# Moving the residual loads, the head stacks and one norm factor within the sliding-window stage of a decoder layer

## The chip, the cores and the metric

The kernel runs on one core of one Trainium2 chip. The time is the device time of one execution in microseconds (us), and the figure that counts is the median of several executions. PE is the matmul engine, DVE the vector engine, ACT the scalar engine, POOL the fourth compute engine, and SP the engine whose queue issues nearly all DMA transfers here. Every engine takes its own instructions strictly in order and waits for others by semaphores.

## The reference

One decoder layer on 512 tokens of width 2048, all in float32:

```
h = RMSNorm(x);  [sb_q|sb_k|sb_v|sw_q|sw_k|sw_v] = h @ w_in
A: 16 heads, causal stick-breaking attention over 512 keys
B: 16 query heads on 4 key heads, window of 128 keys, ALiBi slopes, one learned sink per head
x = x + concat(RMSNorm_A(outA), RMSNorm_B(outB)) @ w_out
x = x + SwiGLU(RMSNorm(x));  out = RMSNorm(x)
```

`outA` and `outB` are 1024 wide each, so `w_out` has a first half of rows that meets `outA` and a second half that meets `outB`. The factor of `RMSNorm_A` is one number per token and can be applied after the product.

## The kernel before

**How products are made.** Float32 operands are split into a rounded high part and the rest (`hi`, `lo`), and each product is three matmuls: hi by hi, hi by lo, lo by hi. A weight tile (a *slab*, 128 x 1024 numbers) is loaded into one of three `raw` buffers by SP, copied to `whi` by ACT (line 219) and subtracted to `wlo` by DVE (line 220).

**The queue of slabs.** All dense products stand in a list `queue`; one entry is one slab with its matmul triples. `step()` emits the next triple; at the first triple of a slab it makes the slab's split and calls its `pre`, and at the third it emits the loads of the next two slabs and the split of the next. `pull(ns)` emits triples until an estimated time is used up, `drain(mark)` emits up to a mark. The attention stages call `pull` between their own steps, so that dense matmuls fill PE while the softmax runs on ACT and DVE. The order of the instructions on each engine is fixed when the program is built; DMA issues keep the order in which the code wrote them.

**The stage around the change.** After the 16 heads of A (64 jobs, lines 952 to 966) come the 16 jobs of B: four *groups* of heads g = 0 to 3, four blocks of 128 queries each. The dense work that fills them is, in the order of the list: four slabs of the value projection V (`add_swv`, on 256-wide matmuls), four slabs of queries for group 2 and four for group 3 (`add_swq`), and then the first half of the output projection in four column *parts* c = 0 to 3 (`add_outA`), four slabs each with 24 matmuls of 512 columns. A part adds its residual: a tile `x2[c]` of 128 x 2048 numbers (1 MB) is loaded from x, and line 1040 adds the part's products to it, scaled by `rstdA`, one DVE instruction for each of four token tiles. The second half (`add_outB`) follows after all jobs.

**A job** (lines 1140 to 1155) has these steps: `swa_exp` (DVE lines 1074 to 1084, ACT lines 1088 and 1089) on the scores of this job; `swa_tr` of the job before (PE transposes line 1110, ACT line 1113, DVE line 1114); `swa_av` of two jobs before (PE lines 1123 and 1124, ACT line 710, DVE line 712); `swa_norm` (DVE lines 1094 to 1102, ACT line 1100); `swa_scores` of the next job (PE lines 1059 and 1060, eight 256-wide matmuls).

**Stacks.** Before its scores a group needs its keys and queries stacked as hi and lo halves: `stack_two` is one ACT and three DVE instructions (lines 696 to 699), `stack_one` one ACT and one DVE instruction (lines 705, 706). `kst[0]` serves groups 0 and 1, `kst[1]` groups 2 and 3.

**Who frees what.** The pool `v8` has four tiles of 8 KB per partition. They hold first the values of A, then the stacks `kst` and `qst`, then the four residual tiles. A residual tile takes the place of a stack, so its load waits until the last scores that read the stack are done: `x2[0]` waits for block 3 of group 1, `x2[1]` for block 3 of group 2, `x2[2]` for block 3 of group 3, and `x2[3]` for nothing more.

**`rstdA`** is the norm factor of A (`sumsq_rstd`): eight small matmuls on the sums of squares `sqA` (line 725), and nine small instructions of DVE and ACT (lines 728 and 276 to 286). It is made between the jobs of A and those of B.

Of the kernel before, what the change touches and what calls it, by code (L numbers as in the profile page):

```python
# [8 lines left out]
F32 = mybir.dt.float32  # L9
# [7 lines left out]
P = 128  # L17
# [20 lines left out]
def tile_hymba(ctx: ExitStack, tc: tile.TileContext, x, ln_mix, w_in, sb_norm, swa_norm,  # L38
# [42 lines left out]
    def four(c):  # L81
        return [pz() for _ in range(NT)] if c % 2 == 0 else [pm(), pm(), po(), po()]
# [639 lines left out]
    def sumsq_rstd(acc, name):  # L722
        pb = po()
        for t in range(NT):
            mm(pb[:, 2 * t:2 * t + 2], lhsT=acc[:, t * P:(t + 1) * P], rhs=ones[:, 0:2],
               start=(t == 0), stop=True, skip_group_check=True)
        sst = sm.tile([P, NT], F32, tag="sst", name="sst")
        V.tensor_copy(out=sst, in_=pb[:, 0:2 * NT].rearrange("p (t two) -> p t two", two=2)[:, :, 0])
        return rstd_from(sst, NT, 1.0 / SBW, name)
# [15 lines left out]
    def sbt(dt, name, n=512, bufs=1):  # L745
        return phase[1].tile([P, n], dt, tag=name, name=name, bufs=bufs)
# [59 lines left out]
    drain_to(11, 0)  # L806
    oA = [o8.tile([P, 4, 512], F32, tag="o8", name="oA") for _ in range(2)]
    kqs = ExitStack()
    kq2 = kqs.enter_context(tc.tile_pool(name="kq2", bufs=1, side="right", reuse_waits="tile")).tile([P, 2, 512], F32, name="kq2")
    add_feat(win, [(C_SWK, 256)], two_m, lambda c, pb: k_evac(pb, kq2[:, c, :]))  # L810
    sb_mark = len(queue)
    add_swv()
# [2 lines left out]
    for name in ("sh3", "sl3", "wh3", "wl3"):  # L815
        z3[name] = sbt(F32R, name, 256)
        G.memset(f(z3[name]), 0.0)
    sqA = sbt(F32, "sqA")

    class Head:  # L820
        pass
# [122 lines left out]
    def at(fn, j):  # L944
        if 0 <= j < NJ:
            fn(*jobs[j])
# [18 lines left out]
        at(sb_lo, j)  # L965
        pull(SBFILL / 3, sb_mark)
    drain(sb_mark)
    rstdA = sumsq_rstd(sqA, "rstdA")


    swp = open_phase("swp", 15)
# [10 lines left out]
    kst = [None, None]  # L982
    qst = [None] * 4

    def stack_keys(c):
        for e in range(2):
            stack_two(kq2[:, c, :], e * HD, kst[c][:, 2 * e, :], kst[c][:, 2 * e + 1, :])

    def stack_queries(g, src):
        for c in range(2):  # L990
            for e in range(2):
                stack_one(src[:, c, :], e * HD, qst[g][:, c * 2 + e, :])

    smarks = [0] * 4

# [10 lines left out]
        smarks[g] = len(queue)  # L1006

    kst[0], qst[0], qst[1], kst[1] = (v8.tile([P, 4, 512], F32R, tag="v8", name=n) for n in ("kst", "qst", "qst", "kst"))
    stack_keys(0)
    stack_queries(0, kq[0][:, 0:2, :])  # L1010
    for g in (2, 3):
        add_swq(g)

# [16 lines left out]
    x2 = [None] * 4  # L1030

    def add_outA(c):
        def banks():
            x2[c] = v8.tile([P, NT, 512], F32, tag="v8", name="x2")
            dma(out=x2[c], in_=x2d[:, c * 512:(c + 1) * 512].rearrange("(t p) c -> p t c", p=P))
            return four(1)

        def done(t, pb):
            xc = x2[c][:, t, :]
            V.scalar_tensor_tensor(out=xc, in0=pb, scalar=rstdA[:, t:t + 1], in1=xc, op0=ALU.mult, op1=ALU.add)  # L1040
        add_tok(lambda s: wout[s * 256:(s + 1) * 256, c * 512:(c + 1) * 512], 4, 2, 512,
                lambda k: mixA[k], banks, done, mix_prep(mixA, oA, 32))

    for c in range(4):
        add_outA(c)
# [87 lines left out]
    blks = {}  # L1133
    jobs = [(g, blk) for g in range(4) for blk in range(NT)]
    NJ = len(jobs)
    SWFILL = 6900.0
    pull(8000.0)
    at(swa_scores, 0)
    stack_queries(1, kq[0][:, 2:4, :])
    for j in range(NJ + 2):  # L1140
        at(swa_exp, j)
        pull(SWFILL / 4)
        at(swa_tr, j - 1)
        pull(SWFILL / 4)
        if j == 2:
            drain(swv_end)
        if j == 3:
            stack_keys(1)
        if j + 1 < NJ and jobs[j + 1][1] == 0:
            drain(smarks[jobs[j + 1][0]])  # L1150
        at(swa_av, j - 2)
        pull(SWFILL / 4)
        at(swa_norm, j)
        at(swa_scores, j + 1)
        pull(SWFILL / 4)
    kqs.close()
    drain()
    rstdB = sumsq_rstd(sqB, "rstdB")


# [687 lines left out]
```

## Time and profile before

| | |
|---|---|
| median of 3 runs | 2029.74 us (2028.69 to 2030.48) |
| the profiled execution's own time | 2027.9 us |
| its span | 2026.2 us |
| PE busy | 1997.1 us, 99% of the span |
| DVE, ACT busy | 1499.1 and 1504.0 us, 74% each |
| last product of A's norm factor to last product of B's (line 725, twice) | 432.85 to 638.72 us |

Times in a profile are from the start of the span. A timeline row gives start, length, engine, line and operands, and in brackets how long the engine had been idle and what ended that. A matmul's length overlaps that of the next, so its cost is the distance between two starts. In a row of the windows, each engine's busy time in the stretch stands with its number of instructions, and after them the TensorE clock granted (1.00 is full speed).

### The profile page before, as it was taken

How to read it: one execution, taken by the hardware profiler on the slowest of the kernel's cores; microseconds unless marked ns; L12 is line 12 of the kernel's file. 1: busy time of each engine (PE TensorE's matmuls, PEld its weight loads, DVE VectorE, ACT ScalarE, POOL GpSimd, SP SyncE). 2: the span in 40 equal slices, each digit the busy share in tenths (PEclk: the TensorE clock that was granted, in tenths of full speed). 3: DMA queues.
4: the chain of work that ended last, by engine and by line, in shares of the span. 5: the costliest groups of instructions: out<-in, count | busy, mean ns of one | idle time of the engine just before them, and what ended most of it. 6: DMA issues, size and time to landing. Idle time of an engine off the chain costs nothing.

```text
span 2026.2 us, 29383 instructions
## 1 busy us (share of the span) xinstructions
PE 1997.1 (99%) x10364; PEld 1703.6 (84%) x10364; DVE 1499.1 (74%) x2038; ACT 1504.0 (74%) x2063; POOL 1104.2 (54%) x597
## 2 busy tenths in 40 slices
PE   9999999989989999999999999999999999999998
PEld 8888888888868888888888888888888888888886
DVE  6667888878864787777777777777777867767767
ACT  6766777766752468777777777777777788878887
POOL 2842444420000047666676666666766678878883
PEclk9999999999989999999999999999999999999999
DMA  6422222212233354544435445354453743533423
GB/s 205 139 60 77 63 67 69 63 53 63 79 118 127 115 177 110 141 107 128 130 105 141 109 126 134 101 141 112 123 137 100 268 161 104 174 138 104 171 89 115
DMA packets 284323, 240.24 MB, mean 119 GB/s; under 512 B 11024, under 2 KB 233296, under 8 KB 281744
## 3 DMA queue, kind: packets, MB, share of 16 engines
q1 hardware_dynamic: 283504, 235.71, 39.0%
q8 instruction: 82, 1.34, 0.3%
q0 software_dynamic: 288, 1.32, 0.2%
q10 hardware_dynamic: 384, 1.34, 0.2%
q14 instruction: 65, 0.53, 0.1%
HBM read 218.40 MB, written 19.92 MB: 118 GB/s over the span
## 4 chain that ended last, share of the span: by engine, by line
PE 74%; DVE 2%; ACT 1%; DMA 1%; issue 0%; POOL 0%; DVEq 0%; ACTq 0%; POOLq 0%
PE o L118 34%; PE m L118 28%; PE m L381 2%; PE m L380 2%; PE m L382 2%; PE o L380 1%; PE o L381 1%; PE o L382 1%; PE z L118 1%; DMA raw<-in_w_out_dram 1%; PE z L1110 0%; PE o L414 0%; PE o L412 0%; PE o L413 0%; PE z L1184 0%
## 5 line engine op out<-in xcount | busy, mean ns | idle before, releaser
L118 DVE TENSOR_TENSOR wlo<-t,hp 128x1024 fp32r<-128x1024 f32 x247 | 301.1, 1219 | 184.9 <-PE o L118 114.3
L118 POOL TENSOR_TENSOR t<-raw,t 128x1024 f32<-128x1024 f32 x111 | 282.5, 2545 | 281.1 <-ACT hp L118 268.9
L118 ACT ACTIVATE whi<-t 128x1024 fp32r<-128x1024 f32 x247 | 262.0, 1061 | 125.9 <-PE o L118 76.0
L118 PE MATMUL o<-hca,whi 128*128 128x512 f32 x880 | 307.6, 391 | 0.0
L118 POOL TENSOR_TENSOR t<-raw,raw 128x1024 f32<-128x1024 f32 x114 | 295.1, 2591 | 22.2 <-issue 11.2
L118 DVE TENSOR_TENSOR wlo<-raw,hp 128x1024 fp32r<-128x1024 f32 x187 | 228.3, 1221 | 91.2 <-issue 51.7
L118 ACT ACTIVATE whi<-raw 128x1024 fp32r<-128x1024 f32 (+1 forms) x189 | 199.8, 1057 | 105.5 <-PE m L118 75.2
L118 ACT ACTIVATE hp<-t 128x1024 fp32r<-128x1024 f32 x247 | 249.1, 1009 | 2.4 <-POOL t L118 2.4
L118 PE MATMUL o<-hca,wlo 128*128 128x256 f32 x880 | 244.3, 280 | 0.0
L118 ACT ACTIVATE hp<-raw 128x1024 fp32r<-128x1024 f32 x191 | 192.8, 1009 | 3.1 <-DVE wlo L118 1.3
L118 PEld LDWEIGHTS o<-hca,whi 128*128 128x128 f32 x880 | 164.3, 187 | 35.5
L118 PE MATMUL m<-hca,whi 128*128 128x512 f32 x528 | 186.4, 392 | 1.1 <-DVE hca L118 1.1
L118 PEld LDWEIGHTS o<-hca,wlo 128*128 128x128 f32 x880 | 165.9, 189 | 0.4
L220 DVE TENSOR_TENSOR wlo<-raw,whi 128x1024 fp32r<-128x1024 f32 x87 | 109.0, 1253 | 72.5 <-ACT whi L219 71.7
L219 ACT ACTIVATE whi<-raw 128x1024 fp32r<-128x1024 f32 x87 | 91.7, 1055 | 94.2 <-PE o L382 45.8
L118 PE MATMUL m<-whi,dca 128*128 128x512 f32 x592 | 146.9, 389 | 0.0
L118 PE MATMUL o<-whi,dca 128*128 128x512 f32 x592 | 146.9, 389 | 0.0
L118 PE MATMUL m<-hca,wlo 128*128 128x256 f32 x528 | 146.5, 280 | 0.0
L412 PE MATMUL m<-hhi,whi 128*128 128x512 f32 x320 | 131.3, 410 | 0.0
L118 PEld LDWEIGHTS o<-whi,dca 128*128 128x128 f32 x592 | 111.1, 188 | 23.1
L118 PEld LDWEIGHTS m<-whi,dca 128*128 128x128 f32 x592 | 111.1, 188 | 23.1
L118 PE MATMUL m<-hcs,whi 128*128 128x512 f32 x352 | 125.9, 392 | 0.0
(386 smaller groups left out, 5265.4 us busy)
## 6 DMA issues: line engine op xcount, KB each, us to landing
raw<-in_w_gate_up_dram SPq DMA_DIRECT2D x348, 256.0 KB, 5.2
raw<-in_w_down_dram SPq DMA_DIRECT2D x68, 512.0 KB, 4.9
raw<-in_w_in_dram SPq DMA_DIRECT2D x35, 512.0 KB, 3.9
raw<-in_w_in_dram SPq DMA_DIRECT2D x66, 256.0 KB, 3.3
raw<-in_w_out_dram SPq DMA_DIRECT2D x32, 512.0 KB, 6.4
aT<-w SPq DMA_DIRECT2D x44, 256.0 KB, 3.4
xd<-aT SPq DMA_DIRECT2D x10, 1024.0 KB, 7.7
rx<-in_w_down_dram SPq DMA_DIRECT2D x20, 512.0 KB, 5.4
```

The lines of the kernel that those rows point to most:

```text
L118: return lambda *a, **k: tc.keep_in_program_order(fn(*a, **k))
L219: A.activation(out=hi, in_=raw, func=AF.Copy)
L220: V.tensor_tensor(out=lo, in0=raw, in1=f(hi), op=ALU.subtract)
L380: mm(o, lhsT=lh[:, sl], rhs=hi[:, j, :], start=first, stop=False, skip_group_check=halves)
L381: mm(o, lhsT=lh[:, sl], rhs=lo[:, j, :], start=False, stop=False, skip_group_check=halves)
L382: mm(o, lhsT=ll[:, sl], rhs=hi[:, j, :], start=False, stop=(k == nslab * a - 1), skip_group_check=halves)
L412: mm(o, lhsT=wh, rhs=xh, start=(k == 0), stop=False)
```

## The change

- The load of the residual tile moves from the `pre` of a part's first slab to the `pre` of its third. The banks for the products are still taken at the first.
- `stack_keys` and `stack_queries` are cut by head and by column pair. Before the first scores, only what group 0 needs is stacked; group 1's queries follow in jobs 0 and 1, the second half of `kst[0]` in job 2, and the two halves of `kst[1]` in jobs 5 and 6 (before: all of `kst[1]` in job 3).
- `rstdA` is made in job 3 and no longer between the two attention stages. `sqA` moves to a pool that outlives the jobs.
- Before the first scores, `pull(16000, ...)` emits slabs of V; the fill per job goes from 6900 to 5800 ns by the kernel's own estimate.
- The final `drain` comes ahead of closing the pool of `kq2` and `sqA`.

```diff
@@
-    kq2 = kqs.enter_context(tc.tile_pool(name="kq2", bufs=1, side="right", reuse_waits="tile")).tile([P, 2, 512], F32, name="kq2")
+    kqp = kqs.enter_context(tc.tile_pool(name="kq2", bufs=1, side="right", reuse_waits="tile"))
+    kq2 = kqp.tile([P, 2, 512], F32, name="kq2")
@@
-    sqA = sbt(F32, "sqA")
+    sqA = kqp.tile([P, 512], F32, name="sqA")
@@
     drain(sb_mark)
-    rstdA = sumsq_rstd(sqA, "rstdA")
+    pull(16000.0, swv_end - 1)
@@
-    def stack_keys(c):
+    def stack_keys(c, e):
+        stack_two(kq2[:, c, :], e * HD, kst[c][:, 2 * e, :], kst[c][:, 2 * e + 1, :])
+
+    def stack_queries(g, c):
         for e in range(2):
-            stack_two(kq2[:, c, :], e * HD, kst[c][:, 2 * e, :], kst[c][:, 2 * e + 1, :])
-
-    def stack_queries(g, src):
-        for c in range(2):
-            for e in range(2):
-                stack_one(src[:, c, :], e * HD, qst[g][:, c * 2 + e, :])
+            stack_one(kq[0][:, 2 * g + c, :], e * HD, qst[g][:, c * 2 + e, :])
@@
-    stack_keys(0)
-    stack_queries(0, kq[0][:, 0:2, :])
+    stack_keys(0, 0)
+    stack_queries(0, 0)
+    stack_queries(0, 1)
@@
     def add_outA(c):
-        def banks():
+        def residual():
             x2[c] = v8.tile([P, NT, 512], F32, tag="v8", name="x2")
             dma(out=x2[c], in_=x2d[:, c * 512:(c + 1) * 512].rearrange("(t p) c -> p t c", p=P))
-            return four(1)
@@
-                lambda k: mixA[k], banks, done, mix_prep(mixA, oA, 32))
+                lambda k: mixA[k], lambda: four(1), done, mix_prep(mixA, oA, 32))
+        queue[-2]["pre"] = residual
@@
-    SWFILL = 6900.0
+    SWFILL = 5800.0
     pull(8000.0)
     at(swa_scores, 0)
-    stack_queries(1, kq[0][:, 2:4, :])
+    stacks = {0: lambda: stack_queries(1, 0), 1: lambda: stack_queries(1, 1), 2: lambda: stack_keys(0, 1),
+              5: lambda: stack_keys(1, 0), 6: lambda: stack_keys(1, 1)}
     for j in range(NJ + 2):
         at(swa_exp, j)
+        if j == 3:
+            rstdA = sumsq_rstd(sqA, "rstdA")
+        if j in stacks:
+            stacks[j]()
...
-        if j == 3:
-            stack_keys(1)
...
-    kqs.close()
     drain()
+    kqs.close()
```

No instruction is added or taken away on any engine; they stand in another order between about 420 and 640 us of the profile.

On SP's queue, at the loads of the output projection, the rows were these (`raw` from `in_w_out` is one weight slab, `x` a residual tile):

```order
L100 DMA raw<-in_w_in_dram 128x4x256 x16
L100 DMA raw<-in_w_out_dram 128x2x512 x2
L100 DMA x_5240<-in_x_dram 128x4x512
L100 DMA raw<-in_w_out_dram 128x2x512 x4
L100 DMA x_5571<-in_x_dram 128x4x512
```

and are now:

```order
L100 DMA raw<-in_w_in_dram 128x4x256 x16
L100 DMA raw<-in_w_out_dram 128x2x512 x4
L100 DMA x_5332<-in_x_dram 128x4x512
L100 DMA raw<-in_w_out_dram 128x2x512 x4
L100 DMA x_5675<-in_x_dram 128x4x512
```

Each residual load stood behind two slabs of its own part, with the other two behind it; now all four slabs of the part stand ahead of it, and the next part's first slab behind it.

On PE, behind the last scores of group 3 (the last row of `kst` and `qst`), which free the third residual tile, there stood transposes of one job, the value products of another, and then the third slab of part 2, whose load waits behind that residual:

```order
L1060 MATMUL z<-kst,qst 128x256
L1110 MATMUL z<-ident,s 128x128 x8
L1123 MATMUL z<-phi,swv 128x512
L1124 MATMUL z<-plo,swv 128x512
L1123 MATMUL z<-phi,swv 128x512
L1124 MATMUL z<-plo,swv 128x512
L380 MATMUL m<-whi,mhi 128x512 x2
```

Now the same scores are followed by 15 matmuls of part 2's last slab, of which the first three are shown,

```order
L1060 MATMUL z<-kst,qst 128x256
L380 MATMUL m<-whi,mhi 128x512
L381 MATMUL m<-wlo,mhi 128x512
L382 MATMUL m<-whi,mlo 128x512
L380 MATMUL o<-whi,mhi 128x512
```

and behind those 15 by the transposes, the value products and part 3's first slab:

```order
L382 MATMUL o<-whi,mlo 128x512
L1110 MATMUL z<-ident,s 128x128 x8
L1123 MATMUL z<-phi,swv 128x512
L1124 MATMUL z<-plo,swv 128x512
L1123 MATMUL z<-phi,swv 128x512
L1124 MATMUL z<-plo,swv 128x512
L380 MATMUL m<-whi,mhi 128x512 x2
```

Behind the last scores of group 2 there stood the same transposes and value products, eight scores and part 1's third slab; now 27 matmuls of part 1's own slabs, the transposes, the value products, eight scores and then part 2's first slab.

On DVE, where the jobs of B begin, the last stacks, the norm factor and the first job stood together:

```order
L706 TENSOR_TENSOR qst<-kq,qst 64x512 x3
L728 COPY sst<-o 128x4
L975 CAST dist<-disti 128x256
L276 TENSOR_SCALAR rv<-sst 128x4
L706 TENSOR_TENSOR qst<-kq,qst 64x512
L282 TENSOR_TENSOR rt<-rr 128x4
L283 TENSOR_TENSOR rt<-rt,rv 128x4
L284 TENSOR_SCALAR rt<-rt 128x4
L286 TENSOR_TENSOR rstdA<-rr,rt 128x4
L1074 SCALAR_TENSOR_TENSOR s<-dist,z 128x128 x4
```

and now the splits of five slabs stand between the last stack and the first job (`wlo`; `swv` is the value stack of V):

```order
L697 CAST kst<-kq_1425 64x512
L698 TENSOR_TENSOR kst<-kq_1425,kst 64x512
L699 CAST kst<-kst 64x512
L220 TENSOR_TENSOR wlo<-raw,whi 128x1024 x2
L272 SCALAR_TENSOR_TENSOR swv<-m,rstd_1275,swv 128x4x64 x4
L220 TENSOR_TENSOR wlo<-raw,whi 128x1024 x3
L1074 SCALAR_TENSOR_TENSOR s<-dist,z 128x128 x4
```

More of the change, by code (lines that the diff above doesn't have):

```diff
@@ L1155, in tile_hymba @@
         pull(SWFILL / 4)
+    drain()
     kqs.close()
-    drain()
     rstdB = sumsq_rstd(sqB, "rstdB")
```

## The prediction

> **What bounds the kernel now.** I read the page first, then PE's idle times in the timeline of 415 to 645 us, the stretch in which the order differs, then the chain of waits there, the windows, and DVE's groups.
>
> ```profile
> PE 1997.1 (99%) x10364; PEld 1703.6 (84%) x10364; DVE 1499.1 (74%) x2038; ACT 1504.0 (74%) x2063; POOL 1104.2 (54%) x597
> ```
>
> PE is busy for 99% of the span, and the change removes no matmul. So it can only win or lose the time in which PE waits, or works at a lower clock, inside the moved stretch. These are PE's rows there with a bracket (those behind the last jobs of A aside), and three score rows as marks:
>
> ```profile
> 432.85 1.05 PE L725 MATMUL o<-ones,sqA 128*128 128x2 f32 x8 [1.45 <-POOL sqA L720]
> 439.97 0.39 PE L381 MATMUL m<-wlo,hhi 128*128 128x256 f32 x1 [2.37 <-DVE wlo L220]
> 488.93 0.41 PE L1110 MATMUL z<-ident,s 128*128 128x128 f32 x2 [0.77 <-DVE s L1102]
> 552.23 0.28 PE L1059 MATMUL z<-kst,qst 128*128 128x256 f32 x1
> 557.01 0.39 PE L1059 MATMUL z<-kst,qst 128*128 128x256 f32 x1 [0.79 <-DVE plo L1114]
> 561.46 1.06 PE L380 MATMUL m<-whi,mhi 128*128 128x512 f32 x2 [3.71 <-ACT whi L219]
> 579.98 0.28 PE L1059 MATMUL z<-kst,qst 128*128 128x256 f32 x1
> 591.49 0.28 PE L1059 MATMUL z<-kst,qst 128*128 128x256 f32 x1
> 593.12 0.39 PE L1059 MATMUL z<-kst,qst 128*128 128x256 f32 x1 [1.00 <-DVE plo L1114]
> 598.02 1.94 PE L1110 MATMUL z<-ident,s 128*128 128x128 f32 x8 [4.16 <-DVE s L1102]
> 602.07 0.97 PE L380 MATMUL m<-whi,mhi 128*128 128x512 f32 x2 [0.40 <-ACT whi L219]
> 638.72 1.05 PE L725 MATMUL o<-ones,sqB 128*128 128x2 f32 x8 [0.39 <-POOL sqB L720]
> ```
>
> To price the losses I need what the same matmuls cost without waits. A 256-wide one costs 0.12 us and a 512-wide one 0.228 (distance of two starts), and eight transposes cost 0.87:
>
> ```profile
> 441.03 0.28 PE L381 MATMUL m<-wlo,hhi 128*128 128x256 f32 x1
> 441.15 0.28 PE L382 MATMUL m<-whi,hlo 128*128 128x256 f32 x1
> 566.59 0.39 PE L380 MATMUL m<-whi,mhi 128*128 128x512 f32 x1
> 566.82 0.39 PE L381 MATMUL m<-wlo,mhi 128*128 128x512 f32 x1
> 528.12 0.87 PE z L1110 x8
> ```
>
> Counting the matmuls between the marks in the order before gives the **loss by stretch**:
> - 432.85 to 552.23 (last scores of group 2): 366 of 512, 196 of 256 and 68 transposes make 114.4 us; the trace takes 119.4. Lost 5.0, and 1.45 in front of it.
> - 552.23 to 579.98 (scores of the second job of group 3): 74, 16 and 16 make 20.5; the trace takes 27.75. Lost 7.25.
> - 579.98 to 591.49 (last scores of group 3): 11.4 against 11.5. Lost 0.1.
> - 591.49 to 638.72: 157, 8 and 16 make 38.4; the trace takes 47.2. Lost 8.8.
>
> Together 22.6 us, of which some 1.4 is no wait: each line 725 row takes 0.9 where I counted 0.2. Most of the rest hangs on two DMA waits:
>
> ```profile
> 553.42 0.37 SPq L100 DMA_DIRECT2D x<-in_x_dram  x1
> 553.88 6.45 DMA raw<-in_w_out_dram
> 560.35 1.07 ACT whi L219
> 593.89 0.37 SPq L100 DMA_DIRECT2D x<-in_x_dram  x1
> 594.35 6.59 DMA raw<-in_w_out_dram
> 600.96 1.06 ACT whi L219
> ```
>
> SP stands at the residual until the group's last scores have freed its tile (they start at 552.23 and at 591.49 and end about 553.3 and 593.8). The weight slab queued behind it is issued only then, lands 6.5 us later, and needs 1.07 us of ACT before PE can go on. PE had 4 us of other work. Behind each wait the clock was low, too:
>
> ```profile
> core 0: us, PE busy (x) PEld busy (x) DVE busy (x) ACT busy (x) POOL busy (x), PEclk, DMA share, GB/s
> 460.00:480.00 20.00, 20.00 (x106) 16.93 (x105) 14.53 (x32) 11.88 (x25) 0.00 (x0) 1.00 0.26 80
> 480.00:500.00 20.00, 19.23 (x99) 15.97 (x98) 19.52 (x48) 16.27 (x39) 0.00 (x0) 1.00 0.18 53
> 500.00:520.00 20.00, 20.00 (x105) 16.98 (x104) 19.69 (x45) 16.20 (x39) 1.30 (x1) 1.00 0.22 72
> 553.00:565.00 12.00, 7.45 (x32) 5.52 (x32) 10.72 (x32) 8.62 (x26) 0.00 (x0) 0.86 0.71 241
> 565.00:592.00 27.00, 27.00 (x139) 22.79 (x137) 15.15 (x34) 11.76 (x27) 1.54 (x2) 1.00 0.03 11
> 592.00:606.00 14.00, 8.44 (x34) 6.42 (x33) 11.31 (x28) 10.69 (x29) 1.02 (x1) 0.76 0.64 211
> ```
>
> ```profile
> 563.60 0.63 PE L382 MATMUL m<-whi,mlo 128*128 128x512 f32 x1
> 564.03 0.63 PE L381 MATMUL m<-wlo,mhi 128*128 128x512 f32 x1
> ```
>
> The granted clock averages 0.86 and 0.76 there, and 512-wide matmuls started 0.43 us apart, half as fast as usual. That is included in the 7.25 and 8.8.
>
> **The change, part by part.**
>
> *The seam between the stages* (stacks, `rstdA`, the first `pull`). Today PE waits 1.45 us for POOL's last sum of squares, since `rstdA` stands in front of everything, and 2.37 us for a slab's `wlo`, which DVE reaches only after the stacks, the norm factor and the first job. Afterwards both are covered by V's slabs: the `wlo` tiles stand ahead of the first job on DVE, and PE reaches the first scores only after some 27 us more of dense work, by the same count. Stacks done while POOL still sums cost more than later ones:
>
> ```profile
> L706 DVE TENSOR_TENSOR qst<-kq,qst 64x512 fp32r<-64x512 f32 x4 | 3.9, 981 | 0.1
> L706 DVE TENSOR_TENSOR qst<-qf,qst 64x512 fp32r<-64x512 f32 x8 | 5.5, 685 | 0.2
> ```
>
> I take back the whole 3.8 us (at least 1.45, if DVE is late after all; POOL's sum is certainly done by job 3).
>
> *The jobs of groups 0 to 2, with less fill.* Here the change costs. From the first job's transposes to the first `wlo` of part 1 the new order has 151 DVE instructions: seven jobs' steps, eight slab splits, the moved stacks, `rstdA`, eight splits of A's output and the first residual addition. In 480 to 520 us, a like mixture, DVE was full: 93 instructions in 39.2 us, 0.42 us each. So DVE needs 63.7 us. PE has 220 matmuls of 512, 64 of 256, 48 transposes and a line 725 row: 63.9 us. Neither leads. In-order DVE then pays for every reply of ACT that comes late, and PE for DVE. Where it was as full before, 480 to 520, PE lost 0.8 us. That is the low bound. The high bound: DVE waits for ACT as it did in the first jobs (`wlo` for `whi` at line 220, and others),
>
> ```profile
> DVE wlo L220 <- ACT whi L219: 8.9, 4, 3.2
> DVE plo L1114 <- ACT phi L1113: 1.7, 1, 1.7
> ```
>
> 10.6 us in 430 to 465, less the slack that a split one slab (5.5 us) ahead gives: some 7 us with the rest. I follow the row of 480 to 520, but over 64 us at full load instead of 40 at 98%, and with stacks and the norm factor's Ln and Exp in ACT's order between the softmax steps: 3.5 us. Of the 5.0 lost before, 0.7 is the line 725 row and 2.4 the seam's, so 1.9 stood here, and 1.6 of my 3.5 is new.
>
> *The residual loads.* The wait itself stays: SP still stands at each residual until the same scores are done, and the first slab of the next part now stands behind it. New is what PE has left to do. From the end of the scores to the first matmul of that slab takes 0.1 + 0.46 (SP's issue of the residual, row to row) + 6.5 + 1.07, so 8.1 to 8.3 us.
> - Behind group 1 ten us of PE's work follow; the residual itself lands 5.3 us after issue (row below) and is needed about as late. DVE adds it in order, with softmax behind. I price this within the 3.5.
> - Behind group 2: 27 and four 512-wide matmuls, eight transposes and eight scores, 7.05 + 0.87 + 0.96 = 8.9 us. The load is covered, but ACT does the next job's four exponentials in front of `whi`, and DVE three residual additions in front of `wlo`. I take 1.3 us lost (0 to 3) in place of 7.25.
> - Behind group 3: 19 matmuls of 512 and eight transposes, 4.32 + 0.87 = 5.2 us. The slab comes 3.1 us too late. Then all four residual additions stand on DVE between the landing and the slab's `wlo`:
>
> ```profile
> DMA to landing us min/median/max: 5.1/5.3/6.7
> L1040 DVE SCALAR_TENSOR_TENSOR x<-o,rstdA,x 128x512 f32<-128x512 f32 x8 | 6.0, 747 | 2.2 <-PE o L382 2.1
> L220 DVE TENSOR_TENSOR wlo<-raw,whi 128x1024 fp32r<-128x1024 f32 x28 | 34.3, 1223 | 28.4 <-ACT whi L219 28.2
> ```
>
> 0.1 + 5.3 + 4 x 0.70 + 1.2 = 9.4 us after the scores, against 6.1 to the slab's first low-part matmul: 3.3 to 3.4 us, at most 4.7 with the 6.7 landing. After idle times of 3.71 and 4.16 us the clock was half for 3 to 5 us, at a loss of about 2; after 2.37 it was full (441.03 to 441.15 is 0.12). A wait of 3.2 lies between; I take 1.0. Together 4.4 (3.1 to 6.7) in place of 8.8 less the 1.1 that B's norm factor keeps.
>
> The Trainium skill, "TensorE: Matmul & The Clock Gate" (Part 1, the HAM clock gate), says that the clock halves after an idle window of about 3.4 us that runs freely and does not start with the wait. By that rule a wait of 3.2 us would never hold a whole window, and the 1.0 would be nothing; the times would come out 1 us lower. The 3.71, 4.16 and 2.37 above agree with it.
>
> `SWFILL` moves no work away: with less fill per job, the rest of the slabs follows behind the jobs, where PE is full anyway (565 to 592 us shows it busy throughout). The closing of the pool after `drain` issues nothing.
>
> **The sum.** Lost after: 0.7 (line 725) + 3.5 + 1.3 + 4.4 + 1.1 = 11.0 us. Before: 22.6. The gain is 11.6 us. Against the profiled execution's own 2027.9 (span 2026.2) that is 2016.3; the median of the runs lies 1.8 above that execution, so I forecast **2018 us**.
>
> **Rivals.**
> - *The seam and the jobs cost nothing* (DVE leads PE, as 14.53 of 20 us busy in 460 to 480 would allow): losses 0.7 + 0.8 + 0 + 3.1 + 1.1 = 5.7, a gain of 17, 2013 us. Against it: 151 instructions at the full rate.
> - *DVE becomes the bound*: 7 in the jobs, 3 behind group 2, 6 behind group 3: with 0.7 and 1.1, 17.8 lost, a gain of 5, 2025 us. For it: DVE's 19.5 of 20 us; against it: 0.77 us lost there.
> - *The moved wait takes the place of the old one*: the next part's slab stalls PE by 7 behind group 2 and 8 behind group 3 as today, and only the seam's 3.8 is won, less 1.6 in the jobs: 2027.5 us, no change. For it: the chain from scores to slab is unaltered. Against it: 8.9 us of work where there were 4.
> - *Slower*: DVE stands at the late residual. If the last scores of a group fall behind so that the residual lands after its part is finished, PE runs out of banks and every softmax step queues behind. From the scores 0.1 + 6.7 + 2.8 + 1.2 = 10.8 us pass, 5.6 more than the 5.2 us of cover, three times, each with 2 us of low clock: 22.8; with 7 in the jobs and 1.8 fixed it is 31.6, 9 more than today, 2039 us. It decides once DVE lies some 4 us behind PE at groups 1 and 2, where cover is 9 to 10 us. Little speaks for it.
>
> **How the numbers follow.** The forecast gets 0.54, the rivals in order 0.20, 0.13, 0.08 and 0.05. About 0.2%, 4 us, can be told from no change, so below 2025.7 counts as faster: the forecast, the first rival and most of the second, 0.86; the same 0.09; slower 0.05. The range is 2012 to 2026: the first rival's losses a little reduced, and the second rival's with 1 us more.
>
> **What would show it.** Right: no bracket over 1 us on PE between the last jobs of A and job 3; no half clock behind group 2's last scores; one wait of 3 to 4 us at part 3's first slab, ended by `whi` or by `wlo`; DVE over 95% busy from job 2 to job 9, with many PE waits under 1 us on lines 1102, 1114 and 220 that sum to 3 to 4 us. Wrong: PE waits above 2 us at parts 1 or 2 (the residual is late on DVE), or above 6 in the jobs, or none at part 3.

## The result, and the profile after

The changed kernel takes **2015.34 us** (median of 4 runs, 2014.66 to 2015.72), the kernel before 2029.59 beside it (2028.69 to 2030.48): a ratio of 0.9929, with a 95% interval of 0.9912 to 0.9947. It is 14.3 us faster; forecast were 11.6 us and 2018. Between the two profiled executions the spans differ by 12.3 us (2026.2 and 2013.9), and that is the number on which the forecast's sum can be tested, since it was made on the profiled execution.

PE's own row of the page of the changed kernel, first of all: the same instructions, 2.2 us less busy, so some 10 of the 12.3 us are waits.

```profile
PE 1994.9 (99%) x10364; PEld 1701.0 (84%) x10364; DVE 1498.8 (74%) x2038; ACT 1502.5 (75%) x2063; POOL 1101.8 (55%) x597
```

PE's timeline of the changed kernel answers to the rows that the prediction showed of before: every row with a bracket of more than 0.35 us from the last job of A on, the first row of the scores of four jobs, and the two norm factors (lines behind 809 can have a number that differs by one to three: line 1040 of the kernel before is line 1039 here).

```profile
427.57 0.50 PE L935 MATMUL o<-l,vst 128*128 128x512 f32 x1
460.07 0.28 PE L1059 MATMUL z<-kst,qst 128*128 128x256 f32 x1
483.71 0.95 PE L725 MATMUL o<-ones,sqA 128*128 128x2 f32 x8
525.24 1.10 PE L1110 MATMUL z<-ident,s 128*128 128x128 f32 x8 [0.57 <-DVE s L1102]
531.67 0.50 PE L381 MATMUL m<-wlo,mhi 128*128 128x512 f32 x1 [0.93 <-DVE wlo L220]
562.94 0.28 PE L1059 MATMUL z<-kst,qst 128*128 128x256 f32 x1
564.41 0.73 PE L380 MATMUL m<-whi,mhi 128*128 128x512 f32 x2 [0.36 <-ACT whi L219]
572.85 0.28 PE L1059 MATMUL z<-kst,qst 128*128 128x256 f32 x1
589.85 0.28 PE L1059 MATMUL z<-kst,qst 128*128 128x256 f32 x1
599.40 0.74 PE L380 MATMUL m<-whi,mhi 128*128 128x512 f32 x2 [3.20 <-ACT whi L219]
626.45 1.02 PE L725 MATMUL o<-ones,sqB 128*128 128x2 f32 x8
```

The seam has no bracket left, and neither has line 725, the norm factors. One large wait remains, 3.20 us at part 3's first slab. The loss by stretch, with the prediction's prices and the matmuls counted between the marks in each order (the marks named in the table are the changed kernel's; from 589.85 to 626.45, for example, 124 of 512, 8 of 256 and 16 transposes make 30.9 us; the trace takes 36.6):

| stretch | before, us lost | after | forecast |
|---|---|---|---|
| seam: from the last row of A's jobs; before, with the 2.37 us at V's slab | 4.1 | 0.3 | 0 |
| line 725 for A (no wait) | 0.7 | 0.7 | 0.7 |
| jobs of groups 0 to 2, with what lies behind group 1 (460.07 to 562.94) | 1.9 | 2.8 | 3.5 |
| behind group 2 (562.94 to 572.85) | 7.25 | 1.0 | 1.3 |
| 572.85 to 589.85 | 0.1 | 0.1 | 0 |
| behind group 3, to B's norm factor (589.85 to 626.45) | 8.8 | 5.7 | 4.4 + 1.1 |
| sum | 22.9 | 10.6 | 11.0 |

The difference of the sums is the 12.3 us of the spans: all of the change's effect lies in this table, none behind it.

What ends the 3.20 us wait stands in the chain of waits (start, length, what) and in SP's rows of the timeline:

```profile
591.00 0.37 SPq L100 DMA_DIRECT2D x<-in_x_dram  x1
591.46 9.54 SPq L100 DMA_DIRECT2D raw<-in_w_out_dram  x4
```

Asked of the slab issued at 591.46 alone (one of the four in that row), the trace gives:

```profile
DMA to landing us min/median/max: 6.3/6.3/6.3
```

```profile
595.75 2.08 ACT s L1088 x8
...
597.92 0.48 ACT phi L1113
598.40 0.96 ACT whi L219
```

SP issues the residual at 591.00, when group 3's last scores end, and the slab at 591.46. The slab lands 6.3 us later, at about 597.7. ACT comes to its `whi` at 598.40, directly behind the last job's exponentials and a `phi`, so ACT's order adds 0.7 us to what the load takes.

The windows show how full DVE was in the jobs,

```profile
500.00:520.00 20.00, 20.00 (x107) 17.01 (x106) 18.25 (x43) 16.09 (x42) 1.29 (x1) 1.00 0.00 1
520.00:540.00 20.00, 18.50 (x96) 15.19 (x95) 19.75 (x53) 13.86 (x35) 0.00 (x0) 1.00 0.46 158
```

(behind the window's length come PE, PEld and then DVE: 18.25 and 19.75 of 20 us), and what the clock did around the wait (PE's busy time stands behind the window's length, the granted clock behind POOL's):

```profile
597.10:600.50 3.40, 1.10 (x4) 0.67 (x4) 3.17 (x5) 3.38 (x9) 0.00 (x0) 1.00 0.80 301
600.50:603.90 3.40, 3.35 (x9) 2.57 (x9) 3.29 (x9) 0.71 (x2) 0.00 (x0) 0.50 0.58 149
603.90:607.30 3.40, 3.40 (x17) 2.80 (x16) 0.26 (x1) 0.84 (x3) 0.00 (x0) 1.00 1.02 374
```

Half clock for 3.4 us, and full again. That half-rate window alone costs 1.7 us, where 1.0 was forecast.

### The profile page after: what moved, and what is told of

Its sections match the earlier page's. It is cut to its first block, busy times and chain, and to the rows that moved or that the text cites. A ratio compares the mean times of both kernels' runs of the same rounds, so it can differ in the third digit from the quotient of the medians.

```text
span 2013.9 us, 29375 instructions
## 1 busy us (share of the span) xinstructions
PE 1994.9 (99%) x10364; PEld 1701.0 (84%) x10364; DVE 1498.8 (74%) x2038; ACT 1502.5 (75%) x2063; POOL 1101.8 (55%) x597
## 4 chain that ended last, share of the span: by engine, by line
PE 95%; DVE 2%; ACT 2%; issue 1%; DMA 0%; POOL 0%; SPq 0%; DVEq 0%; ACTq 0%; POOLq 0%
PE o L118 36%; PE m L118 30%; PE m L412 4%; PE m L413 3%; PE m L414 3%; PE m L381 2%; PE m L382 2%; PE m L380 2%; PE z L118 1%; PE o L381 1%; PE o L382 1%; PE o L380 1%; PE o L935 0%; PE o L934 0%; PE z L851 0%
```

## The experiments

Three questions were open: whether the 14 us come from the residual's place or from the seam; what exactly sets the cost of a residual load; and why the clock fell.

The experiments were run in three rounds; the kernel before, run beside them, took 2028.8, 2029.6 and 2029.6 us there, so differences of less than 1 us between kernels of different rounds mean little.

**The residual's place alone.** The kernel before with only this edit:

```diff
-        def banks():
+        def residual():
             x2[c] = v8.tile([P, NT, 512], F32, tag="v8", name="x2")
...
-            return four(1)
...
-                lambda k: mixA[k], banks, done, mix_prep(mixA, oA, 32))
+                lambda k: mixA[k], lambda: four(1), done, mix_prep(mixA, oA, 32))
+        queue[-2]["pre"] = residual
```

> The kernel before, with one part of the change alone: the residual is loaded at a part's third slab. The seam, the stacks and the fill of 6900 stay as they were. My theory (a residual load costs what the slab behind it lacks in cover): in this order the slab behind x2[1] (part 2's first) comes 12.98 us of PE work after the last scores of group 2, against 8.2 us that load and split need, so the 7.25 us lost there fall to about 0.3; the slab behind x2[2] (part 3's first) comes 4.51 us after the last scores of group 3, so a wait of about 3.8 us stays, with about 2.5 us of low clock and low-part delay, 6.4 lost in place of 8.8. The seam's 1.45 and 2.37 stay. Gain 9.4 us: 2020. Rival 1 (the seam and the spreading of the stacks bring most of the 14 us, the residual little): 2025 or more. Rival 2 (the residual brings everything): 2015.

Measured: 2019.43 us (2019.22 to 2020.9) against 2028.84, ratio 0.9956 (0.9941 to 0.9971). The gain is 9.4 us, as forecast from the covers. The seam's two waits stand as before, part 2's wait is gone, and part 3's is there with its 3.8 us:

```profile
439.86 0.51 PE L381 MATMUL m<-wlo,hhi 128*128 128x256 f32 x1 [2.38 <-DVE wlo L220]
603.41 0.91 PE L380 MATMUL m<-whi,mhi 128*128 128x512 f32 x2 [3.75 <-ACT whi L219]
```

**All the rest alone.** The changed kernel with the residual at the first slab:

```diff
-        def residual():
+        def banks():
             x2[c] = v8.tile([P, NT, 512], F32, tag="v8", name="x2")
...
+            return four(1)
...
-                lambda k: mixA[k], lambda: four(1), done, mix_prep(mixA, oA, 32))
-        queue[-2]["pre"] = residual
+                lambda k: mixA[k], banks, done, mix_prep(mixA, oA, 32))
```

> The changed kernel with the residual load put back to a part's first slab: the other parts of the change alone. My theory: the two pulls ahead of the jobs (24 us of V) bring the output projection forward, so that all three residuals come too early. The slabs behind them come 0.87, 1.90 and 1.78 us of PE work after the last scores that free the tile, against 8.2 us needed: waits of 7.3, 6.3 and 6.4 us, each with 2 us of half clock, 26 us, and some 3.5 for the rest; 29.5 lost where the kernel before loses 22.9. Slower than before by some 6 us: 2036. Rival (the parts add up: the seam is worth what the change brings beyond the residual, 4 to 5 us): 2025.

Measured: 2035.40 us (2034.21 to 2037.10), ratio 1.0034 (1.0022 to 1.0047). Slower, as the covers say. Three loads stall where two did, one per group:

```profile
524.82 0.45 PE L1110 MATMUL z<-ident,s 128*128 128x128 f32 x1 [6.33 <-DVE s L1102]
563.76 0.44 PE L1110 MATMUL z<-ident,s 128*128 128x128 f32 x1 [4.02 <-DVE s L1102]
606.05 0.45 PE L1110 MATMUL z<-ident,s 128*128 128x128 f32 x1 [4.41 <-DVE s L1102]
521.80:528.60 6.80, 3.75 (x12) 3.06 (x13) 6.70 (x17) 3.81 (x6) 0.00 (x0) 0.50 0.83 293
```

Each is followed or accompanied by 6.8 us of half clock (the last row, from the windows, is the first of the three). So the parts do not add up: the residual's place wins 9.4 alone, the rest loses 6.6 alone, and together they win 14.3. The two pulls, 24 us by the kernel's own estimate, pull the output projection forward, and the residuals with it: in the changed kernel the first scores come 32.5 us after the last row of A's jobs (427.57 to 460.07), in the kernel before 7.7 us.

**Only one pull.** The changed kernel without its second pull:

```diff
-    pull(8000.0)
     at(swa_scores, 0)
```

> The changed kernel without its second pull (8000 ns by the kernel's estimate) in front of the first scores; the 16000 stays. Everything behind the seam moves some 8 us of PE work later against the jobs. My theory: part 2's and part 3's first slabs then come some 17 and 13 us of PE work after the scores that free the tile ahead of them on SP's queue, both over 8.3, so the 5.7 us lost behind group 3 and the 1.0 behind group 2 go, and 16 us of V still cover the seam: 2015.3 - 6.4 = 2009. Rival (DVE is what holds the jobs; less fill ahead only moves the wait to another place): 2014 to 2016, with waits of PE for DVE that sum to as much. Rival 2 (the seam opens again: waits of 1 to 4 us at the first scores or at V's slabs): 2011 to 2013.

Measured: **2007.03 us** (2006.79 to 2007.83), ratio 0.9894 (0.9880 to 0.9907) to the kernel before, and 8.3 us below the changed kernel. That is 2 us more than I had forecast, and the fastest kernel of this study. Between the last job of A and B's norm factor a single wait of PE is left:

```profile
522.86 0.41 PE L1110 MATMUL z<-ident,s 128*128 128x128 f32 x2 [0.23 <-DVE s L1102]
```

The rival in which DVE holds the jobs falls with it: DVE is at 19.2, 19.7 and 19.4 of 20 us from 480 to 540 us there, against 18.3, 18.3 and 19.8 in the changed kernel, and PE loses almost nothing. In the trace the one pull puts 10.9 us ahead of the first scores (426.96 to 437.85).

**The fourth corner: one pull, and the residual at the first slab.**

```diff
-    pull(8000.0)
     at(swa_scores, 0)
...
-                lambda k: mixA[k], lambda: four(1), done, mix_prep(mixA, oA, 32))
-        queue[-2]["pre"] = residual
+                lambda k: mixA[k], banks, done, mix_prep(mixA, oA, 32))
```

> The kernel with one pull ahead of the jobs, and the residual load put back to a part's first slab: the fourth corner beside the changed kernel (2015.3), the one without the residual's move (2035.4) and the one with one pull (2007.0). My theory (loss = what the slab behind a residual lacks in cover, and the half clock behind the wait): the slabs behind the three loads come 8.88, 6.15 and 2.46 us of PE work after the scores, against 8.2 us needed: nothing, a wait of 2.1 us (perhaps with 1.7 us of half clock) and one of 5.8 us with 1.7 to 3.4 us of half clock: 11 us more than one pull, 2018 (2016 to 2020). Rival (the place of the load matters as much as it did with two pulls, 20 us): 2027. Rival 2 (with one pull the place of the load does not matter): 2007.

Measured: 2022.42 us (2021.28 to 2023.38), ratio 0.9965 (0.9951 to 0.9979). That is 4.4 us more than forecast, outside my range and about halfway to the first rival's 2027. The second and the third wait are where my theory puts them; the first was not expected:

```profile
520.64 0.73 PE L380 MATMUL m<-whi,mhi 128*128 128x512 f32 x2 [1.69 <-ACT whi L219]
556.09 0.72 PE L380 MATMUL m<-whi,mhi 128*128 128x512 f32 x2 [2.00 <-ACT whi L219]
593.20:600.10 6.90, 6.35 (x14) 4.62 (x15) 3.23 (x6) 2.90 (x7) 0.00 (x0) 0.51 0.70 232
```

The second wait is as forecast. The first, 1.69 us, was to be nothing with 8.88 us of cover; in the chain of that kernel ACT does a job's four exponentials (eight instructions with their sums) and two splits of A's output in front of the slab's `whi`:

```profile
516.36 1.22 ACT mhi L271 x2
517.58 0.79 ACT s L1088 x3
518.37 1.18 ACT s L1088 x5
519.64 0.95 ACT whi L219
```

So the 8.2 us that a slab needs behind a residual are a lower bound; ACT's order can add 2. And behind the third wait (5.01 us) the clock was half for two windows, while PE had work for 6.35 of 6.9 us.

In a table, medians in us:

| | residual at the first slab | at the third |
|---|---|---|
| before's pull (8000, behind the first scores) and fill 6900 | 2029.6 | 2019.4 |
| two pulls, fill 5800 | 2035.4 | 2015.3 (the change) |
| one pull, fill 5800 | 2022.4 | **2007.0** |

(The first row has the old seam, the others the new one.) The later load is worth about 10, 20 and 15 us.

**The fill per job.**

```diff
-    SWFILL = 5800.0
+    SWFILL = 6900.0
```

> The changed kernel with the fill per job back at 6900. My theory: the output projection runs ahead of the jobs; the slabs behind the three residuals come 2.94, 1.55 and 1.78 us of PE work after the scores, against 8.2 needed, so waits of 5.3, 6.7 and 6.4 us come back with 2 to 3 us of half clock each, although the load stands at the third slab: 2033 (2030 to 2037). Rival (the residual at the third slab is what counts, whatever the fill): 2014 to 2018, DVE having less time per job.

Measured: 2037.79 us (2036.59 to 2038.54), ratio 1.0040 (1.0025 to 1.0055). Of all edits this one moves the most: 22 us, with the residual at its new place. That is 0.8 us above the range of my theory. The waits return: 5.0 us on `whi` in three and 7.4 on line 1102 in two; two more, 2.25 us at line 1123 and 3.90 us at line 1110, are for softmax steps of DVE and ACT, and the second of them ends before the third residual is issued. The low clock after group 2 lasts 10.2 us, three times 3.4; that is where I had 2 to 3:

```profile
570.55 0.66 PE L1110 MATMUL z<-ident,s 128*128 128x128 f32 x2 [4.01 <-DVE s L1102]
569.20:579.60 10.40, 8.00 (x24) 6.42 (x25) 9.57 (x19) 6.19 (x15) 0.00 (x0) 0.51 0.75 276
```

**One slab later still.**

```diff
-        queue[-2]["pre"] = residual
+        queue[-1]["pre"] = residual
```

> The changed kernel with the residual loaded at a part's fourth slab in place of its third. The next part's first slab then stands ahead of the residual on SP's queue, its second behind. My theory (the 3.20 us wait hangs on the order of SP's queue): part 3's first slab is there in time; what PE waits for is a bank, which is free when the residual, issued at 591.0, has landed (5.1 us) and two additions are done: 597.6, a wait of about 1.6 us in place of 3.20 and no half clock; its second slab has 10.65 + 1.6 us of cover. 3.7 us won there and about 0.5 behind group 2: 2011. Rival (ACT's exponentials and DVE's additions in front of the split set the wait, not the queue): 2014 to 2015.5.

Measured: 2009.70 us (2009.59 to 2010.14), ratio 0.9902 (0.9888 to 0.9917), 5.6 us below the changed kernel. Part 3's first slab is there in time; PE now waits for a bank, which the first residual addition frees (line 1039), and the clock stays full. It waits 0.90 us where I expected 1.6, since one addition is enough:

```profile
595.45 0.50 PE L380 MATMUL m<-whi,mhi 128*128 128x512 f32 x1 [0.90 <-DVE x L1039]
```

The rival's 2014 to 2015.5 did not come. But with the slab loaded ahead of the residual its split stands ahead of the last job's exponentials, too, so this run alone does not tell SP's order from ACT's. The landing in the changed kernel does: of the 3.20 us, 0.7 are ACT's order, as shown above, and the rest is SP's queue and the load. DVE's additions add nothing there: they are done at 599.15, and the slab's `wlo` starts at 599.38, behind `whi`.

**Useless work in front of the wait.** The value products of one job, PE's last work ahead of the 3.20 us, done twice and then three times:

```diff
-        for j in range(nk):
+        for j in [j for _ in range(2 if (g, blk) == (3, 1) else 1) for j in range(nk)]:
```

> The changed kernel with useless work: the four value products of group 3's second job are computed twice (the second time starting the sum anew, so the result is the same). They are PE's last work in front of its 3.20 us wait for part 3's first slab. My theory (the 2.1 us of half clock behind that wait come of its length): 0.91 us more of work leave the end of the wait where it is, 599.40, and make the idle time 2.3 us, after which the clock stays full, as it did after 2.37 us in the kernel before: about 2 us faster, 2013.3. Rival (the clock falls for another reason, for example because the slab's first matmuls come slowly): no change, 2015.3. Rival 2 (the work is not hidden): 2016.2.

Measured: 2015.47 us (2014.60 to 2016.24), ratio 0.9934 (0.9922 to 0.9947). No gain: here my theory fell. The wait is shorter, but the clock is halved all the same:

```profile
599.65 0.73 PE L380 MATMUL m<-whi,mhi 128*128 128x512 f32 x2 [2.26 <-ACT whi L219]
597.40:600.80 3.40, 1.15 (x4) 0.67 (x4) 3.17 (x6) 3.38 (x9) 0.00 (x0) 1.00 0.81 306
600.80:604.20 3.40, 3.33 (x9) 2.62 (x9) 3.29 (x9) 0.80 (x2) 0.00 (x0) 0.52 0.51 146
```

The kernel with the residual alone showed the same thing: its 2.38 us wait at the seam was followed by half clock, although the 2.37 us at the same place in the kernel before were not. These are the windows of the one, and then of the other:

```profile
436.40:439.80 3.40, 1.08 (x10) 0.88 (x8) 3.40 (x13) 0.64 (x1) 0.00 (x0) 1.00 0.00 0
439.80:443.20 3.40, 3.34 (x16) 3.34 (x17) 3.39 (x11) 2.25 (x11) 0.00 (x0) 0.52 0.56 160
```

```profile
435.40:438.80 3.40, 2.21 (x19) 2.00 (x17) 3.27 (x15) 1.76 (x2) 0.59 (x1) 1.00 0.00 0
438.80:442.20 3.40, 2.23 (x18) 2.23 (x19) 3.39 (x8) 1.75 (x9) 0.00 (x0) 1.00 0.32 87
592.40:595.80 3.40, 0.73 (x4) 0.53 (x4) 3.30 (x11) 3.16 (x10) 0.62 (x1) 1.00 0.21 23
```

In the kernel before the half clock began at 561.67 and at 595.80, ten windows of 3.413 us apart. Counted back from there by 3.413 us, an edge falls at 438.8, in the middle of the 2.37 us wait: each side had PE busy for 2.2 us. In the other kernel the half clock began at the wait's end, 439.8, so one window held the whole wait. This gave a new theory, and the third run:

> The changed kernel with the four value products of group 3's second job computed three times (the result is the same), 1.82 us of useless work in front of the wait for part 3's first slab. With them twice the wait fell from 3.20 to 2.26 us and the clock was half all the same, from 600.8 to 604.1. The stretches of half clock in all traces so far last 3.4 us or twice that, and began 0.1 to 1.0 us behind the wait's end. New theory: the clock is judged over free-running windows of 3.4 us and is halved after a window in which PE idled 2.3 us or more; a window need not be idle throughout. Three times leave a wait of 1.35 us, as a stretch of 1.2 us of idle time in a window left the clock full in the kernel before: full clock, 2013.6. Rival (any wait there of a microsecond, or the slow start of the slab, halves it): 2015.4, with half clock to about 604.

Measured: 2013.46 us (2013.32 to 2013.98), ratio 0.9921 (0.9906 to 0.9936). With 1.82 us of useless work the kernel is 1.9 us *faster*, and the half clock is gone:

```profile
599.25 0.73 PE L380 MATMUL m<-whi,mhi 128*128 128x512 f32 x2 [1.33 <-ACT whi L219]
595.35:598.76 3.41, 2.57 (x12) 1.72 (x10) 3.34 (x7) 3.20 (x12) 0.00 (x0) 1.00 0.98 360
598.76:602.18 3.42, 2.87 (x11) 2.08 (x12) 3.14 (x6) 1.98 (x3) 0.00 (x0) 1.00 0.43 124
```

These two windows are this execution's own. Its clock next falls at 2005.05 us, at the end of PE's work, and 412 windows of 3.4133 us counted back from there put an edge at 598.76, so the wait is cut in two and PE is busy for 2.57 and 2.87 us. A window that holds the whole wait, 597.40 to 600.80 for one, would still have PE busy for 2.00 us. The full clock of this one execution therefore has two possible reasons, the shorter wait and where the window fell; that the four times lie within 0.7 us of each other speaks for the wait.

**The seam's three edits.** First the norm factor back between the stages:

```diff
+    rstdA = sumsq_rstd(sqA, "rstdA")
     pull(16000.0, swv_end - 1)
...
-        if j == 3:
-            rstdA = sumsq_rstd(sqA, "rstdA")
```

> The changed kernel with A's norm factor made between the stages again, as before; the rest as changed. My theory (the seam's 1.45 us are PE waiting for POOL's last sum of squares): a wait of 1.4 us at line 725 comes back, the two pulls cover everything behind it, and the rest moves with it: 2015.3 + 1.4 = 2016.8. Rival (other work hides it): 2015.3.

Measured: 2018.31 us (2017.17 to 2019.84), ratio 0.9942 (0.9925 to 0.9960). The wait came back as forecast, the time did not: 1.5 us above my 2016.8.

```profile
432.66 1.05 PE L725 MATMUL o<-ones,sqA 128*128 128x2 f32 x8 [1.39 <-POOL sqA L720]
430.20:433.60 3.40, 2.01 (x18) 1.81 (x17) 2.93 (x3) 0.63 (x1) 2.02 (x2) 1.00 0.50 154
433.60:437.00 3.40, 3.40 (x18) 3.40 (x18) 3.05 (x9) 0.73 (x3) 1.14 (x2) 0.51 0.00 0
```

Its price, 3.0 us, is 1.6 us more than the wait, about what one window of half clock costs. Its four times are 2017.17, 2017.24, 2019.38 and 2019.84, and the profiled one, 2019.38, has half clock from 433.6 to 437.0: the wait and eight products of two columns lie in one window.

Then the stacks as they were, with the pulls as changed:

```diff
     stack_keys(0, 0)
+    stack_keys(0, 1)
     stack_queries(0, 0)
     stack_queries(0, 1)
+    stack_queries(1, 0)
+    stack_queries(1, 1)
...
-    stacks = {0: ..., 1: ..., 2: ..., 5: ..., 6: ...}
+    stacks = {3: lambda: [stack_keys(1, e) for e in range(2)]}
```

> The changed kernel with the stacks where they were: those of groups 0 and 1 all ahead of the first scores, the second heads' keys in the fourth job. Norm factor, pulls, fill and residual as changed. My theory (24 us of V cover DVE ahead of the first scores, so the spreading of the stacks carries none of the 2.37 us; the pull does): no wait at the seam, 2015.3 with 0.5 us either way. Rival (stacks in one piece hold up DVE's splits for V): waits of 2 to 4 us at V's slabs, 2017.5 to 2019.

Measured: 2017.05 us (2016.29 to 2019.18), ratio 0.9941 (0.9923 to 0.9959). The time lies above the 0.5 us either way that I allowed. Still, PE has no wait at V's slabs, so the pulls alone cover DVE's stacks there. The span of the profiled execution is 0.7 us longer than the changed kernel's, the median 1.7 us; the intervals of the two ratios overlap, so whether the spreading earns anything stays open.

Then the new pull away, the old one kept:

```diff
-    pull(16000.0, swv_end - 1)
```

> The changed kernel without the new pull of 16000 in front of the jobs; the one of 8000 stays, which the order puts behind the first scores. My theory: no residual holds up a slab (part 0 is not yet at its third slab when group 1's scores are done), so 8.3 us are won as with one pull (2007.0), but PE is at the first scores 5 us behind the last jobs of A and finds the stacks unfinished, and then V's third slab not split: waits of 1.5 and 2 to 3 us: 2011 (2010 to 2013). Rival (the stacks, now spread, need no cover): 2007.

Measured: 2012.99 us (2012.86 to 2014.72), ratio 0.9919 (0.9904 to 0.9935). No residual stalls, and the seam is open:

```profile
438.30 0.38 PE L381 MATMUL m<-wlo,hhi 128*128 128x256 f32 x1 [3.81 <-DVE wlo L220]
436.00:439.40 3.40, 1.10 (x9) 1.10 (x10) 3.40 (x9) 0.98 (x5) 0.00 (x0) 1.00 0.01 1
439.40:442.90 3.50, 3.50 (x19) 3.50 (x19) 2.99 (x12) 2.05 (x10) 0.00 (x0) 0.51 0.82 251
```

One wait of 3.81 us, not two, and 1.7 us of half clock that I had left out; the spread stacks do not make a pull needless. But this kernel is 2.4 us faster than the changed one: on top of the old pull, the new one costs more at the residual loads than it wins at the seam.

At last the three edits that the runs leave as the effective ones, on the kernel before:

```diff
     rstdA = sumsq_rstd(sqA, "rstdA")
+    pull(16000.0, swv_end - 1)
...
-    pull(8000.0)
-    SWFILL = 6900.0
+    SWFILL = 5800.0
...
+        queue[-2]["pre"] = residual
```

> The kernel before with three edits alone: the residual at the third slab, a pull of 16000 right behind A's norm factor in place of the 8000, and a fill of 5800 per job. Stacks and norm factor stay where they were. My theory: as with one pull (2007.0), plus the 1.4 us for POOL's sum ahead of the norm factor: 2008.5. Rival (the spread stacks and the late norm factor each earn their place): 2011 or more.

Measured: 2009.14 us (2008.75 to 2011.65), ratio 0.9901 (0.9885 to 0.9917). Its span is 1.7 us longer than that of the kernel with one pull (2007.2 and 2005.5), and two waits make that up:

```profile
432.10 1.05 PE L725 MATMUL o<-ones,sqA 128*128 128x2 f32 x8 [1.28 <-POOL sqA L720]
489.99 1.24 PE L1111 MATMUL z<-ident,s 128*128 128x128 f32 x8 [0.46 <-DVE s L1103]
```

So the late norm factor is worth about 1.3 us, and the spread stacks, if the second wait is theirs, half a microsecond.

## Why the prediction was right, and where it was not

**The seam** ("I take back the whole 3.8 us"): right, 4.1 lost before and 0.3 after. By the runs, the late norm factor removes POOL's wait (1.39 us when it is put back) and the pull removes the one at V's slab (3.81 us without it). That the stacks' new places take part in it is not shown.

**The jobs** (3.5 us, bounds 0.8 to 7): measured 2.8, by another picture than the one I drew. I expected DVE over 95% busy from job 2 on with many small waits. It was 91% busy from 500 to 520 with PE full, and its waits came at one place, 520 to 540, 0.57 and 0.93 us (the other 1.3 us of the 2.8 stand in no bracket), in front of which the chain of waits is DVE alone for 12 us: the second heads' keys, a job's steps, a residual addition and the split of part 1's first slab. The run with one pull shows that DVE can be 97% busy for 60 us and cost PE almost nothing.

**Behind group 2** (1.3 us, 0 to 3): measured 1.0, of which 0.36 is the wait for `whi`.

**Behind group 3** (4.4 us and 1.1 for B's norm factor): measured 5.7 in all. The wait was forecast at 3.1 for the slab's `whi` and at 3.3 to 3.4 by way of DVE's four additions, and was 3.20, ended by `whi`; the additions were done 0.2 us ahead of it. Two terms beside it were off, and that they nearly cancel is luck. B's norm factor waits for nothing any more (POOL is done when PE gets there), so the 0.39 us wait in its 1.1 is gone; the other 0.7, the length of the row, begins only at the mark and never stood in this stretch, before or after. And the clock, put at 1.0 between nothing and 2, was half for a whole 3.4 us, 1.7 us, with some 0.8 of small delays at the slab beside it.

For the clock term I had set beside it the rule of the Trainium skill, "TensorE: Matmul & The Clock Gate" (Part 1, the HAM clock gate), that the clock halves after an idle window of about 3.4 us, and had concluded that a wait of 3.2 us would never hold a whole one. The runs agree with the length of the window and that it runs freely: half clock lasted 3.4, 6.8 and 10.2 us, and began by the window, not by the wait. They do not agree that the window has to be idle: PE was busy for 1.10 of the 3.4 us ahead of the half clock in the changed kernel, and for 1.15 with the value products twice. Nor does the 4.16 us wait of the kernel before agree, as I had thought: its half clock began at 595.80, in the middle of the wait, behind a window with PE busy for 0.73 us, and lasted 6.8 us, not 3 to 5.

**From the profile to the median.** The rest of the miss, 2 of 2.7 us, is in none of these terms. I added 1.8 us because the median of before lay above its profiled execution; the changed kernel's median lies 0.3 below its own (2015.62). A wait of the right length costs 1.7 us of half clock in one execution and nothing in another, and that would explain such a difference. The record bears it out for the kernel before, whose 24 runs beside the experiments spread over 2027.0 to 2032.0 us: the twelve with a mean granted clock of 0.996 took 2027.0 to 2029.5, the six with 0.995 took 2028.6 to 2030.6, and the six with 0.994 or 0.993 took 2029.8 to 2032.0 (one window of half clock lowers that mean by 0.0008). Three kernels in which no half clock is left in the stretch (one pull, the fourth slab, three times the value products) spread over 0.6 to 1.0 us. A fourth, the one with three edits, has none in its profiled execution either, but one of its other runs is over 2 us longer than the rest, at 0.998 against 0.999. Which wait was hit in which run is not shown, since single runs were not profiled.

**The rivals.** That all is free was too bright for this kernel, but holds for the one with one pull: 2007. The slower one named the right danger, a residual that comes before the jobs are ready for it, with the wrong trigger: not DVE's lag, but PE's lead in the output projection decides. With the fill at 6900 it happened at 2037.8 us, near the 2039 of that rival. What I did not ask was whether the change takes too much fill: I worked out the cover of 5.2 us behind group 3 and took it as given, though removing the second pull was the simplest way to raise it.

## What to carry to other kernels

A load that waits for a buffer stalls everything behind it on its queue, so the number to work out is the cover: the matmul time between the work that frees the buffer and the first use of what is queued behind. It depends on how far the filler has run ahead as much as on where the load is written; here the same edit was worth about 10, 20 or 15 us, and more filler made the kernel slower by 22. If a wait of two to four microseconds cannot be removed, count the clock with it, and look whether work can be put in front of it: here 1.82 us of useless work won 1.9 us, and half as much won nothing.

## What the runs showed of the hardware that I had not expected

- The granted clock falls window by window, of 3.413 us, by how long PE was busy in the last one. Most windows shown above stand up to 0.2 us off; placed by each trace's own changes of the clock, PE was busy for 0.73 (the kernel before), 1.04 (the residual alone), 1.09 (the changed kernel), 1.18 (no new pull) and 1.22 us (value products twice) ahead of half clock, and for 1.45 at the end of PE's work with the value products three times (2001.64 to 2005.05). It was busy for 1.67 (fill 6900, the row below; the next window, to 535.13, was at full clock), 1.69 (one pull, residual at the first slab), 1.82 (no new pull) and twice 2.23 us (the kernel before) where the clock stayed full. The bound lies between 1.45 and 1.67 us of 3.41.

```profile
528.30:531.72 3.42, 1.67 (x8) 1.29 (x8) 3.38 (x8) 0.00 (x0) 0.00 (x0) 1.00 1.02 356
```

- What brings the clock back is not settled by these runs: with one pull and the residual at the first slab it stayed half behind a window with PE busy for 3.02 us (593.36 to 596.77), and in the kernel before it came back behind one with 3.02 us (599.21 to 602.63).
- The windows run freely: 2.37 and 2.38 us of waiting at the same place left the clock full in one kernel and halved it in another.
- PE's busy time in the records is not quite what counts: 1.39 us of waiting halved the clock where 1.05 us of eight two-column products followed. The window of 430.23 to 433.65 us there has PE busy for 2.03 us, 1.1 without them, and of the windows of these traces with more than 1.67 us busy at full clock it is the only one that half clock followed. In the kernel with three edits 1.28 us and the same products left it full; counted by that trace's own change of the clock (2002.33), an edge at 432.19 parts the wait from nearly all of the products, and the window with the wait (428.78 to 432.20) has PE busy for 2.13 us, so that run does not contradict it. That such small products count for little is my reading; no run isolates it.
